# Two-layer encoder in float32 on one core: the first head group kept on chip through the paired gate projections and rotated behind them, and stored gates loaded two at a time on the weights' queue

## The chip, the cores and the metric

The kernel runs on one core of one Trainium2 chip. The metric is the device time of one execution in microseconds (us). The engines are named as in the profile: PE (TensorE, matmuls), PEld (its weight loads), DVE (VectorE), ACT (ScalarE), POOL (GpSimd) and SP (SyncE, which here only issues transfers).

## The reference

An encoder trunk of two layers on 512 tokens of width 2048; 16 meta tokens go ahead of them, so 528 rows are worked on. Only layer 0, attention, is touched by the change.

```python
def attention_mixer(h, w_in, q_norm, k_norm, w_out, ang_row, ang_col):
    proj = h @ w_in
    q, k, v, gate = jnp.split(proj, [...], axis=-1)
...
    q = apply_axial_rope(rmsnorm(q, q_norm), ang_row, ang_col)
    k = apply_axial_rope(rmsnorm(k, k_norm), ang_row, ang_col)
...
    s = jnp.einsum('bqkgd,bskd->bkgqs', qb, k) * (ATTN_HEAD_DIM ** -0.5)
    p = jax.nn.softmax(s.astype(jnp.float32), axis=-1).astype(v.dtype)
    o = jnp.einsum('bkgqs,bskd->bqkgd', p, v)
...
    return (o * jax.nn.silu(gate)) @ w_out

for i in range(2):
    y = rmsnorm(h, pre_norm[i])
    y = attention_mixer(...) if i == 0 else gla_mixer(...)
    h = h + rmsnorm(y, post_norm[i])
return h[:, 16:]
```

There are 16 query heads of 128 in 8 groups; the two heads of a group share one k and one v. A group thus takes four projections of 128 columns (k, q0, q1, v), and each head has a gate projection of 128 columns besides. Layer 1 is a chunked gated linear attention with a gate of its own.

## The kernel before, in words

**Arithmetic.** Every float32 operand is split into a high and a low part (`split`, L128: ACT makes the high part, DVE the low one), and a product is three matmuls (L152 to L154). The normalised rows lie on chip as `uh`, `ul`, features on the partitions and the 528 rows along the free axis, in two halves of 264. A 128-column projection (`project`) is 16 feature tiles by two halves by three matmuls, 96 matmuls of 128x264. Its weights come in two loads of 512 KB on SP's queue into two raw buffers (`weights`, L141) and are split into three pairs `whi`, `wlo`.

**Order.** `Clock` (L38) is a clock for writing the program out: each feature tile of a projection moves it on by 3*(264+7)/2400, some 10.8 for a whole projection, and generators and `clk.after` calls put the other work between at set times. A scheduler then fixes each engine's order from that; loads of weights are drawn ahead of other work.

**Stages.** With x coming in, PE accumulates k, q0 and q1 of group 0 in six PSUM banks, to about 60 us. Then `taken` copies each out, scaled by its norm's weight, and squares it, and `rope` (L297) rotates it, one after the other, with `clk.flush()` between them. `rope` sends four swapped quarters from `qw` to `qs` (L301, on SP), splits the square, multiplies on POOL by cos and sin (L306, L307), sums the square over the partitions by two matmuls on ones for each half into one PSUM bank (L311, L312; its result is taken by DVE at L313), takes the inverse root on ACT, adds and scales on DVE (L318, L319), and splits the result. Under that stand four projections: gates 0 to 2 and v of group 0, all stored in DRAM (`to_dram`). Then `combine` (L193) builds on DVE, in 8 steps, sums of the four quarters of `uh + ul` into `th`, `tl`, and `seven` (L206) makes two gate projections at a time from seven products of such sums instead of eight: five pairs, gates 3 to 12, stored in DRAM. Its first pair is written in another order (`late=True`), which puts a product of plain `u` second.

**Attention.** `attention` takes a group in nine steps (`SLOTS` of clock each): scores and softmax, then transposes, then, by `clk.after`, `weighted` (L659), the product with v into the bank "o". That bank is a pool of one buffer (`ps_o`), and `rope`'s row sums use it too. While a group is attended, the next group's k, q0, q1 and v are projected and rotated (`qkv`); the second half's row sums come 6.5 behind the projection, in `late`. From group 1 on `stored_gates` (L595) brings the two gates of the group before: GpSimd loads one into `gr` (two buffers), DVE multiplies by `rrow` (L604), `silu` takes ACT and POOL (L614), DVE multiplies the result onto the attention's output (L608), and only then comes the second gate's load. The eight groups run from about 230 to 800 us. The output projection and layer 1 follow.

Of the kernel before, what the change touches and what calls it, by code (L numbers as in the profile page):

```python
# [9 lines left out]
F32 = mybir.dt.float32  # L10
# [8 lines left out]
P = 128  # L19
# [14 lines left out]
AHEAD = 400  # L34
SLOTS = (3.8, 3.8, 3.8, 3.8, 3.8, 3.8, 3.8, 2.6)

# [45 lines left out]
def hybrid_encoder(  # L82
# [21 lines left out]
    g_d = scratch.tile([13, P, T], F32, name="g_d")  # L104
    v0_d = scratch.tile([P, T], F32, name="v0_d")
    kq_d = scratch.tile([4, P, T], F32, name="kq_d")
# [98 lines left out]

    def seven(src, c, ys, th, tl, free, late=False):  # L206


# [27 lines left out]
        def add(o, ps, y):  # L236
            V.tensor_tensor(o, ps, y, op=ALU.add)
# [16 lines left out]
        A.copy(y1[:, l], product(w, of_u(0, 0)))  # L254
        if late:
            w = parts(a12)
            A.copy(y2[:, l], product(w, of_u(1, 0)))
        add(y1[:, r], product(parts(a11), of_t(T2)), y1[:, l])
        if late:
            add(y1[:, l], y1[:, l], y2[:, l])  # L260
        add(y2[:, r], product(parts(a21), of_t(T3)), y1[:, r])
# [3 lines left out]
        add(y1[:, r], p5, y1[:, r])  # L265
        if not late:
            w = parts(a12)
        sums(a11, a12, a11)
        if not late:
            add(y1[:, l], product(w, of_u(1, 0)), y1[:, l])  # L270
        add(y1[:, r], product(parts(a11), of_u(1, 1)), y1[:, r])
# [15 lines left out]
    def take(wcol):  # L287

        qw = wk.tile([P, T], F32, tag="qw", name="qw", bufs=2)
        sq = wk.tile([P, T], F32, tag="sq", name="sq", bufs=1 if wk is ws else 2)  # L290

        def evac(ps, a, b):
            A.activation(qw[:, a:b], ps, AF.Copy, scale=wcol)
            A.activation(sq[:, a:b], ps, AF.Square)
        return qw, sq, evac

    def rope(qw, sq, outs, ps_q, tag):  # L297
        qs = wk.tile([P, T], F32, tag="qs", name="qs", bufs=1)
# [8 lines left out]
        G.tensor_tensor(qs, qs, sin, op=ALU.mult)  # L307

        def sums(a, b):
            ps = ps_q.tile([P, 512], F32, tag=tag, name="ssq")[:, :b - a]  # L310
            PE.matmul(ps, ones_r, sh[:, a:b], start=True, stop=False)  # L311
            PE.matmul(ps, ones_r, sl[:, a:b], start=False, stop=True)  # L312
            V.scalar_tensor_tensor(f[:, a:b], ps, 1.0 / P, erow[:, a:b], op0=ALU.mult, op1=ALU.add)  # L313

        def late():
            sums(*HALVES[1])
            rsqrt_inplace(f)
            V.tensor_tensor(qw, qw, qs, op=ALU.add)  # L318
# [13 lines left out]
    Q1 = T + META  # L332
    qks = [qk_tiles(c0, 0)]

    st = ExitStack()
    sp = pool(st, "start")
    wk = ws = pool(st, "wk_s", 2)
    s2 = pool(st, "start2", 2)
# [136 lines left out]
    V.tensor_scalar(col(QN), col(QN), SCALE, None, op0=ALU.mult)  # L475

    def taken(i):
        qw, sq, evac = take(col(QN if i else KN))
        for j, ps, a, b in banks:
            if j == i:  # L480
                evac(ps, a, b)
        return qw, sq
    head0 = taken(0)

# [12 lines left out]
    rsqrt_inplace(rrow)  # L497
    cos, sin = [ws.tile([P, T], F32, name=n, bufs=1) for n in ("cos0", "sin0")]
    nc.sync.dma_start(out=cos, in_=rope_cos)
    nc.sync.dma_start(out=sin, in_=rope_sin)  # L500
# [14 lines left out]

    def to_dram(dst, i, c):

        y = yp.tile([P, T], F32, tag=f"y{i % 2}", name="y")
        project(w_in0, c, HALVES, lambda ps, a, b: A.copy(y[:, a:b], ps))
        nc.gpsimd.dma_start(out=dst, in_=y)  # L520
    built = clk.drive(combine(th, tl, quarters))
    for i, (dst, c) in enumerate([(g_d[i], 4096 + i * P) for i in range(3)] + [(v0_d, 3072)]):
        to_dram(dst, i, c)
    clk.finish(built)
    free = [wpool.tile([P, 1024], F32, tag="wraw", name="wraw", bufs=2) for _ in range(2)]
    free += [q[:, :1024] for q in quarters]
    for h in range(3, 13, 2):
        ys = y_tiles()
        free = seven(w_in0, 4096 + h * P, ys, th, tl, free, h == 3)
        for i in range(2):  # L530
            nc.gpsimd.dma_start(out=g_d[h + i], in_=ys[i])
# [5 lines left out]
    pk = pool(l0, "pk0")  # L537
    qks.append(qk_tiles(pk, 1))
    pb = pool(l0, "pb0")
# [19 lines left out]
    def values(g):  # L559
        vh = wa.tile([P, 4, P], F32R, tag="vh", name="vh")  # L560
        vl = wa.tile([P, 4, P], F32R, tag="vl", name="vl")
        vm = vm_bufs[g % 2]
        vt = wa.tile([P, T], F32, tag="vt", name="vt", bufs=1)
        if g == 0:
            with tc.high_priority(AHEAD):
                nc.sync.dma_start(out=vt, in_=v0_d)
        else:
            project(w_in0, 3072 + g * P, HALVES, lambda ps, a, b: A.copy(vt[:, a:b], ps))

        def late():  # L570
# [3 lines left out]
            for t in range(4):  # L574
# [22 lines left out]
    def stored_gates(hs, held):  # L597

        yield 6.0
        for h in hs:  # L600
            gr = wa.tile([P, T], F32, tag="gr", name="gr", bufs=2)
            nc.gpsimd.dma_start(out=gr, in_=g_d[h])
            yield 6.0
            V.tensor_tensor(gr, gr, rrow, op=ALU.mult)  # L604
            gs = silu(gr)
            yield 4.0
            og = held[h % 2]
            V.tensor_tensor(og, og, gs, op=ALU.mult)  # L608
            nc.gpsimd.dma_start(out=og_d[h], in_=og)
# [96 lines left out]
    for g in range(KV):  # L706
        o_sb = o_tiles()
        att = attention(qk, vv, o_sb, SLOTS[g])
        att = clk.drive(att)
        gates = [] if g == 0 else [2 * g - 2, 2 * g - 1]  # L710
# [10 lines left out]
        if g + 1 < KV:  # L721
# [6 lines left out]

    slots = [wk.tile([P, T], F32, tag=tag, name="ogr", **kw) for tag, kw in
             (("qw", {}), ("qw", {}), ("qs", dict(bufs=1)), ("sq", dict(bufs=2)))]  # L730
    slots.append(wa.tile([P, T], F32, tag="vt", name="ogr", bufs=1))
    NS = len(slots)
# [696 lines left out]
```

## Time and profile before

| what | value |
|---|---|
| time, median of 3 runs | 1833.05 us (1831.9 to 1833.15) |
| the profiled execution's own time | 1830.58 us |
| its span | 1828.7 us |
| PE busy | 1764.1 us, 96% of the span |
| DVE, ACT, POOL busy | 61%, 52%, 12% |

A row of the timeline gives start, duration, engine, line, operation, output and inputs, shape, count and, in square brackets, how long the engine was idle ahead of it and what ended that. A row of the groups gives busy time, mean ns, and the idle time ahead. A row of the windows gives the window, its length, PE's busy time with its matmuls in brackets, the granted clock (1.00 is full), the share of the transfer engines and GB/s. A row of the waits gives total, times and the longest.

### The profile page before, as it was taken

Reading aid. Unit: us, or ns where it says so; the run is one execution under the profiler, and the core shown is the slowest. Engines: PE = TensorE matmul, PEld = TensorE weight load, DVE = VectorE, ACT = ScalarE, POOL = GpSimd, SP = SyncE. Lnnn points to the kernel's source line nnn. Section 1 sums busy time; section 2 is a strip of 40 time slices with the busy share of each in tenths; the row PEclk is TensorE's granted clock in tenths of the full one; section 3 lists DMA queues with packets and bytes.
Section 4 is the critical chain, followed back from the end, with each engine's and each line's share of the span. In section 5 each row is a group of like instructions: output and inputs, shape, how many; then the busy total and the mean of one; then the engine's idle time right before and its main releaser. Section 6 shows DMA issues by size and latency. Waiting matters only on the chain. (4 is left out here: it accounts for less than half of the span.)

```text
span 1828.7 us, 31700 instructions
## 1 busy us (share of the span) xinstructions
PE 1764.1 (96%) x12591; PEld 1661.6 (91%) x12591; DVE 1118.0 (61%) x1904; ACT 951.1 (52%) x1910; POOL 214.6 (12%) x284
## 2 busy tenths in 40 slices
PE   8969998999989999999999999999999999999998
PEld 8969998999989999999999999998898988888886
DVE  5597765666656666752228697768585775764224
ACT  5633355555555554553237634458575775763221
POOL 3200112122121111021111101110010100000000
PEclk9989999999999999999999999999999999999999
DMA  8334342323232323253335344443332332354323
GB/s 266 115 99 124 113 138 77 87 78 101 66 102 65 88 81 96 72 175 93 93 104 169 118 133 128 125 119 95 87 110 77 102 103 75 104 156 164 101 93 127
DMA packets 266468, 202.03 MB, mean 110 GB/s; under 512 B 9836, under 2 KB 239920, under 8 KB 265792
## 3 DMA queue, kind: packets, MB, share of 16 engines
q1 hardware_dynamic: 255056, 163.33, 30.9%
q0 software_dynamic: 11264, 36.68, 5.8%
q8 instruction: 99, 1.62, 0.4%
q14 instruction: 49, 0.40, 0.1%
HBM read 165.20 MB, written 28.28 MB: 106 GB/s over the span
## 5 line engine op out<-in xcount | busy, mean ns | idle before, releaser
L152 PE MATMUL pp<-uh,whi 128*128 128x264 f32 (+1 forms) x2320 | 713.7, 308 | 3.2 <-DVE gr L620 1.4
L153 PE MATMUL pp<-ul,whi 128*128 128x264 f32 (+1 forms) x2320 | 704.0, 304 | 1.4 <-DVE ul L428 1.4
L154 PE MATMUL pp<-uh,wlo 128*128 128x264 f32 (+1 forms) x2320 | 704.0, 303 | 0.4 <-POOL wlo L367 0.3
L130 DVE TENSOR_TENSOR wlo<-wraw,whi 128x1024 fp32r<-128x1024 f32 (+1 forms) x239 | 293.1, 1228 | 307.8 <-ACT whi L129 306.9
L152 PEld LDWEIGHTS pp<-uh,whi 128*128 128x128 f32 x2320 | 439.1, 189 | 19.8 <-DVE gr L620 1.6
L154 PEld LDWEIGHTS pp<-uh,wlo 128*128 128x128 f32 x2320 | 438.7, 189 | 17.5 <-POOL wlo L367 0.6
L153 PEld LDWEIGHTS pp<-ul,whi 128*128 128x128 f32 x2320 | 439.3, 189 | 15.5 <-DVE ul L428 1.8
L129 ACT CAST whi<-wraw 128x1024 fp32r<-128x1024 f32 (+1 forms) x239 | 248.6, 1041 | 298.0 <-PE pp L153 109.4
L230 PE MATMUL pp<-uh,whi 128*128 128x264 f32 x264 | 75.8, 287 | 13.8 <-ACT whi L129 13.8
L129 ACT CAST whi<-x 128x1024 fp32r<-128x1024 f32 x48 | 50.2, 1047 | 72.6 <-PE pp L231 52.8
L232 PE MATMUL pp<-uh,wlo 128*128 128x264 f32 x264 | 75.7, 287 | 0.0
L1341 PE MATMUL f<-whi,ul 128*128 128x512 f32 x192 | 75.6, 394 | 0.0
L1339 PE MATMUL f<-whi,uh 128*128 128x512 f32 x192 | 75.5, 393 | 0.0
L634 ACT ACTIVATE pn<-s,mx 128x528 f32<-128x528 f32 (+1 forms) x72 | 50.3, 698 | 48.3 <-DVE mx L631 47.5
L231 PE MATMUL pp<-ul,whi 128*128 128x264 f32 x264 | 75.4, 285 | 0.0
L1340 PE MATMUL f<-wlo,uh 128*128 128x512 f32 x192 | 75.3, 392 | 0.0
L130 DVE TENSOR_TENSOR wlo<-x,whi 128x1024 fp32r<-128x1024 f32 x48 | 58.6, 1223 | 20.8 <-ACT whi L129 20.7
L631 DVE TENSOR_REDUCE mx<-s 128x1 f32<-128x528 f32 (+1 forms) x72 | 50.8, 705 | 24.6 <-PE s L628 23.1
L306 POOL TENSOR_TENSOR qw<-qw,cos 128x528 f32<-128x528 f32 x24 | 31.7, 1320 | 276.5 <-DMA qs<-qw 276.5
L230 PEld LDWEIGHTS pp<-uh,whi 128*128 128x128 f32 x264 | 50.3, 191 | 14.0 <-ACT whi L129 14.0
L649 DVE TENSOR_TENSOR pl<-pT,ph 128x512 fp32r<-128x512 f32 (+1 forms) x80 | 47.5, 594 | 22.7 <-ACT ph L648 22.3
L648 ACT CAST ph<-pT 128x512 fp32r<-128x512 f32 (+1 forms) x80 | 40.9, 511 | 37.0 <-PE pT L644 25.8
(399 smaller groups left out, 3714.0 us busy)
## 6 DMA issues: line engine op xcount, KB each, us to landing
wraw<-in_attn_w_in_dram SPq DMA_DIRECT2D x82, 512.0 KB, 4.2
wraw<-in_gla_w_in_dram SPq DMA_DIRECT2D x81, 512.0 KB, 3.9
wraw<-in_attn_w_out_dram SPq DMA_DIRECT2D x32, 512.0 KB, 3.9
wraw<-in_gla_w_out_dram SPq DMA_DIRECT2D x32, 512.0 KB, 3.8
x<-in_gla_w_in_dram SPq DMA_DIRECT2D x15, 512.0 KB, 4.4
qs<-qw SPq DMA_DIRECT2D x96, 66.0 KB, 2.8
x<-in_attn_w_in_dram SPq DMA_DIRECT2D x12, 512.0 KB, 4.2
x<-h_d SPq DMA_DIRECT2D x32, 132.0 KB, 4.0
```

The costliest lines, as they stand in the source:

```text
L129: A.copy(hi, src)
L130: V.tensor_tensor(lo, src, hi.bitcast(F32), op=ALU.subtract)
L152: PE.matmul(ps, wh, uh[:, k, a:b], start=first, stop=False)
L153: PE.matmul(ps, wh, ul[:, k, a:b], start=False, stop=False)
L154: PE.matmul(ps, wl, uh[:, k, a:b], start=False, stop=last)
L230: PE.matmul(ps, w[0][:, k], bh[:, k], start=k == 0, stop=False)
L231: PE.matmul(ps, w[0][:, k], bl[:, k], start=False, stop=False)
L232: PE.matmul(ps, w[1][:, k], bh[:, k], start=False, stop=k == KH - 1)
L631: V.reduce_max(mx, s, axis=AX.XY, negate=True)
L1339: PE.matmul(ps, uh[:, k, ts], wh[:, kk], start=(k == 0), stop=False)
L1340: PE.matmul(ps, uh[:, k, ts], wl[:, kk], start=False, stop=False)
L1341: PE.matmul(ps, ul[:, k, ts], wh[:, kk], start=False, stop=(k == KT - 1))
```

## The change

Group 0's raw k, q0 and q1 are copied from the six banks into three tiles of `c0`, which live through the pairs (`qws`); raw v goes into `vt` there and not to DRAM. The rotation of group 0 leaves the start: `first_group` squares, scales and rotates the three behind the pairs, as a lead-in to the first group's attention, with the row sums 2.6 and 3.9 behind each. The later groups rotate in the same three tiles. Their two row sums are placed apart, at 4.4 and 5.6, and no longer in `late`. Group 1's v is projected ahead of its k. `seven` has one order. The first two groups' slots are 3.0 and 3.5. The two stored gates of a group are both issued at the head of the group, on SP's queue, which also carries the weights. `qs` has two buffers instead of one.

```diff
-SLOTS = (3.8, 3.8, 3.8, 3.8, 3.8, 3.8, 3.8, 2.6)
+SLOTS = (3.0, 3.5, 3.8, 3.8, 3.8, 3.8, 3.8, 2.6)
...
-        qw = wk.tile([P, T], F32, tag="qw", name="qw", bufs=2)
-        sq = wk.tile([P, T], F32, tag="sq", name="sq", bufs=1 if wk is ws else 2)
+        qws.append(qws.pop(0))
+        qw = qws[-1]
+        sq = wk.tile([P, T], F32, tag="sq", name="sq")
...
         def late():
-            sums(*HALVES[1])
             rsqrt_inplace(f)
...
-        clk.after(4.4, lambda: sums(*HALVES[0]))
+        for step, part in zip(steps, HALVES):
+            clk.after(step, lambda part=part: sums(*part))
         clk.after(6.5, late)
...
+    qws = [c0.tile([P, T], F32, name=f"qw{i}") for i in range(3)]
+    vt = c0.tile([P, T], F32, name="vt")
...
-    head0 = taken(0)
+    for i, ps, a, b in banks:
+        A.copy(qws[i][:, a:b], ps)
...
-    for i in range(3):
-        rope(*(taken(i) if i else head0), qks[0][1][i], ps_t, "t")
-        clk.flush()
...
-        clk.after(1.2 if g else 8.0, late)
+        clk.after(1.2 if g else 2.0, late)
...
+        vv = values(g) if g == 1 else None
         for i, c in enumerate((2048 + g * P, 2 * g * P, (2 * g + 1) * P)):
             qw, sq, evac = take(col(KN if i == 0 else QN))
             project(w_in0, c, HALVES, evac)
-            rope(qw, sq, outs[i], ps_o, "o")
-        return qk, values(g)
+            rope(qw, sq, outs[i], (4.4, 5.6))
+        return qk, vv or values(g)
+
+    def first_group():
+        for i in range(3):
+            sq = wk.tile([P, T], F32, tag="sq", name="sq")
+            A.activation(sq, qws[i], AF.Square)
+            A.activation(qws[i], qws[i], AF.Copy, scale=col(QN if i else KN))
+            rope(qws[i], sq, qks[0][1][i], (2.6, 3.9))
+            yield 4.2 if i < 2 else 7.5
 
     def stored_gates(hs, held):
 
+        grs = [wa.tile([P, T], F32, tag="gr", name="gr") for _ in hs]
+        for gr, h in zip(grs, hs):
+            nc.sync.dma_start(out=gr, in_=g_d[h])
         yield 6.0
-        for h in hs:
-            gr = wa.tile([P, T], F32, tag="gr", name="gr", bufs=2)
-            nc.gpsimd.dma_start(out=gr, in_=g_d[h])
-            yield 6.0
+        for gr, h in zip(grs, hs):
+            yield 5.0
             V.tensor_tensor(gr, gr, rrow, op=ALU.mult)
...
-        att = clk.drive(att)
+        lead = first_group() if g == 0 else iter([6.5] if g == 1 else [])
+        att = clk.drive(chain(lead, att))
```

The same change in the engines' orders, at three places. First DVE at the end of the start, before: `x_` are the quarter buffers of `combine`, `qw` the vector being rotated, `wlo` the low part of weights.

```order
L318 TENSOR_TENSOR qw<-qw,qs 128x528
L319 TENSOR_TENSOR qw<-qw,sq 128x528
L130 TENSOR_TENSOR wlo<-wraw,whi 128x1024
L130 TENSOR_TENSOR ql_98<-qw,qh_97 128x512
L130 TENSOR_TENSOR ql_98<-qw,qh_97 128x16
L198 TENSOR_TENSOR x_843<-uh,ul 128x1056
L198 TENSOR_TENSOR x_844<-uh,ul 128x1056
```

The same place now; `rrow` is the copy of the rows' scale that before stood ahead of the first rotation's work.

```order
L130 TENSOR_TENSOR wlo<-wraw,whi 128x1024 x2
L469 TENSOR_SCALAR cols<-cols 128x1
L482 COPY rrow<-mrow 128x512
L483 COPY rrow<-mrow 128x16
L198 TENSOR_TENSOR x_745<-uh,ul 128x1056
L484 TENSOR_SCALAR erow<-rrow 128x528
L200 TENSOR_TENSOR x_745<-x_745 128x528
```

The sums of `combine` (L198 on) now follow the row scale at once; before, the three rotations stood between.

Second, DVE in the third group's attention (376 to 448 us in the profile), where q1 of the fourth group is rotated, before: `gr` is a stored gate, `sq` takes the row sums, `pl` and `pmt` are transposed probabilities.

```order
L608 TENSOR_TENSOR o_sb<-o_sb,gs 128x528
L130 TENSOR_TENSOR sl<-sq,sh 128x528
L649 TENSOR_TENSOR pl<-pT,ph 128x4x128
L651 TENSOR_TENSOR pmt<-pTm,pmt 16x128
L313 SCALAR_TENSOR_TENSOR sq<-ssq,erow 128x264
L604 TENSOR_TENSOR gr<-gr,rrow 128x528
L318 TENSOR_TENSOR qw<-qw,qs 128x528
L313 SCALAR_TENSOR_TENSOR sq<-ssq,erow 128x264
L319 TENSOR_TENSOR qw<-qw,sq 128x528
```

And the same part of the same group now (L306 is now the row sums' line, L590 the gate's multiplication, L310 the adding of `qs`, L594 the product with the gate).

```order
L130 TENSOR_TENSOR sl<-sq,sh 128x528
L594 TENSOR_TENSOR o_sb<-o_sb,gs 128x528
L635 TENSOR_TENSOR pl<-pT,ph 128x4x128
L637 TENSOR_TENSOR pmt<-pTm,pmt 16x128
L306 SCALAR_TENSOR_TENSOR sq<-ssq,erow 128x264
L590 TENSOR_TENSOR gr<-gr,rrow 128x528
L306 SCALAR_TENSOR_TENSOR sq<-ssq,erow 128x264
L310 TENSOR_TENSOR qw_96<-qw_96,qs 128x528
L311 TENSOR_TENSOR qw_96<-qw_96,sq 128x528
```

The second row sum has moved ahead of the adding of `qs`; the gate's multiplication still stands between the two sums. The fourth and fifth groups read the same; in the first two the gate's multiplication now stands behind both sums, and in the last three there is none in either kernel's order.

Third, DVE early in the first group's attention, now (before, nothing is rotated for group 0 there): `qw_94` is k, `qw_95` is q0, `vl` the low part of a group's v.

```order
L130 TENSOR_TENSOR sl<-sq,sh 128x528
L553 SCALAR_TENSOR_TENSOR vl<-vps,rcol,vh 128x128
L310 TENSOR_TENSOR qw_94<-qw_94,qs 128x528
L311 TENSOR_TENSOR qw_94<-qw_94,sq 128x528
L306 SCALAR_TENSOR_TENSOR sq<-ssq,erow 128x264
L130 TENSOR_TENSOR kl_2380<-qw_94,kh_2379 128x528
L306 SCALAR_TENSOR_TENSOR sq<-ssq,erow 128x264
L310 TENSOR_TENSOR qw_95<-qw_95,qs 128x528
L590 TENSOR_TENSOR gr<-gr,rrow 128x528
L130 TENSOR_TENSOR wlo<-wraw,whi 128x1024
```

k's adding of `qs` (L310) stands ahead of both row sums of q0, and a gate's multiplication that belongs to the next group stands behind them.

More of the change, by code (lines that the diff above doesn't have):

```diff
@@ L1 @@
 import heapq
+from itertools import chain
 from contextlib import ExitStack
@@ L104, in hybrid_encoder @@
     g_d = scratch.tile([13, P, T], F32, name="g_d")
-    v0_d = scratch.tile([P, T], F32, name="v0_d")
     kq_d = scratch.tile([4, P, T], F32, name="kq_d")
@@ L204, in combine, with seven @@
             yield 2.4
-    def seven(src, c, ys, th, tl, free, late=False):
+    def seven(src, c, ys, th, tl, free):
         def quarter(t, i, j):
@@ L265, in seven @@
         add(y1[:, r], p5, y1[:, r])
-        if not late:
-            w = parts(a12)
+        w = parts(a12)
         sums(a11, a12, a11)
-        if not late:
-            add(y1[:, l], product(w, of_u(1, 0)), y1[:, l])
+        add(y1[:, l], product(w, of_u(1, 0)), y1[:, l])
         add(y1[:, r], product(parts(a11), of_u(1, 1)), y1[:, r])
@@ L295, in take, with rope @@
         return qw, sq, evac
-    def rope(qw, sq, outs, ps_q, tag):
-        qs = wk.tile([P, T], F32, tag="qs", name="qs", bufs=1)
+    def rope(qw, sq, outs, steps):
+        qs = wk.tile([P, T], F32, tag="qs", name="qs")
         for b in range(4):
@@ L309, in sums @@
         def sums(a, b):
-            ps = ps_q.tile([P, 512], F32, tag=tag, name="ssq")[:, :b - a]
+            ps = ps_o.tile([P, 512], F32, tag="o", name="ssq")[:, :b - a]
             PE.matmul(ps, ones_r, sh[:, a:b], start=True, stop=False)
@@ L475, in hybrid_encoder @@
     V.tensor_scalar(col(QN), col(QN), SCALE, None, op0=ALU.mult)
[L477 to L482, printed above, removed]
-    head0 = taken(0)
+    for i, ps, a, b in banks:
+        A.copy(qws[i][:, a:b], ps)
     V.reduce_sum(ss, ssq, axis=AX.X)
@@ L497, in hybrid_encoder @@
     rsqrt_inplace(rrow)
-    cos, sin = [ws.tile([P, T], F32, name=n, bufs=1) for n in ("cos0", "sin0")]
-    nc.sync.dma_start(out=cos, in_=rope_cos)
-    nc.sync.dma_start(out=sin, in_=rope_sin)
-    for i in range(3):
-        rope(*(taken(i) if i else head0), qks[0][1][i], ps_t, "t")
-        clk.flush()
     st.close()
@@ L514, in y_tiles @@
         return [yp.tile([P, T], F32, tag=f"y{i}", name=f"y{i}") for i in range(2)]
[L516 to L520, printed above, removed]
     built = clk.drive(combine(th, tl, quarters))
-    for i, (dst, c) in enumerate([(g_d[i], 4096 + i * P) for i in range(3)] + [(v0_d, 3072)]):
-        to_dram(dst, i, c)
+    for h in range(3):
+        y = yp.tile([P, T], F32, tag=f"y{h % 2}", name="y")
+        project(w_in0, 4096 + h * P, HALVES, lambda ps, a, b: A.copy(y[:, a:b], ps))
+        nc.gpsimd.dma_start(out=g_d[h], in_=y)
+    project(w_in0, 3072, HALVES, lambda ps, a, b: A.copy(vt[:, a:b], ps))
     clk.finish(built)
@@ L528, in hybrid_encoder @@
         ys = y_tiles()
-        free = seven(w_in0, 4096 + h * P, ys, th, tl, free, h == 3)
+        free = seven(w_in0, 4096 + h * P, ys, th, tl, free)
         for i in range(2):
@@ L537, in hybrid_encoder @@
     pk = pool(l0, "pk0")
-    qks.append(qk_tiles(pk, 1))
+    qks = [qk_tiles(pk, i) for i in range(2)]
     pb = pool(l0, "pb0")
@@ L562, in values @@
         vm = vm_bufs[g % 2]
[L563 to L567, printed above, removed]
+        if g:
             project(w_in0, 3072 + g * P, HALVES, lambda ps, a, b: A.copy(vt[:, a:b], ps))
@@ L726, in hybrid_encoder @@
     last_gs = [gate(14)]
-    slots = [wk.tile([P, T], F32, tag=tag, name="ogr", **kw) for tag, kw in
-             (("qw", {}), ("qw", {}), ("qs", dict(bufs=1)), ("sq", dict(bufs=2)))]
-    slots.append(wa.tile([P, T], F32, tag="vt", name="ogr", bufs=1))
+    slots = qws + [vt] + [wk.tile([P, T], F32, tag=tag, name="ogr") for tag in ("qs", "sq")]
     NS = len(slots)
```

7 lines of the change are left out of this document (removed).

## The prediction

> **What bounds the kernel now.** I read the page first, then the waits of PE, then the rows around the longest of them. The page's busy times say that PE is the resource.
>
> ```profile
> PE 1764.1 (96%) x12591; PEld 1661.6 (91%) x12591; DVE 1118.0 (61%) x1904; ACT 951.1 (52%) x1910; POOL 214.6 (12%) x284
> PE   8969998999989999999999999999999999999998
> ```
>
> PE is busy 96% of the span, and the change takes no matmul away: both programs have the same matmuls by count. So it can only gain what PE waits, and the stretches where PE runs slowly. The waits of PE, longest first:
>
> ```profile
> PE o L664 <- DVE sq L313: 20.5, 7, 4.3
> PE pp L230 <- ACT whi L129: 13.8, 1, 13.8
> PE ssq L311 <- ACT sh L129: 3.0, 2, 1.7
> PE pp L152 <- ACT sq L294: 0.7, 1, 0.7
> ```
>
> Two of these hold most of it: one wait of 13.8 at the first pair, and seven waits in attention, one in each group that projects the next, up to 4.3. (The attention of a group takes some 72 us from 232 on; I call these windows 1 to 8, window 1 being the first group's.) The change touches the places of all four. The first pair, in PE's timeline, where the second product waits:
>
> ```profile
> 112.16 0.28 PE L230 MATMUL pp<-uh,whi 128*128 128x264 f32 x1
> ...
> 129.75 0.59 PE L230 MATMUL pp<-uh,whi 128*128 128x264 f32 x1 [13.79 <-ACT whi L129]
> ...
> 299.38 0.56 PE L664 MATMUL o<-ph,vh 128*128 128x272 f32 x1 [4.32 <-DVE sq L313]
> ```
>
> The projections end at 112.16 and the pair begins; its weights for the second product sit in a buffer that `combine` works in until the end, and `combine` is DVE's. DVE's timeline there, and its groups from 92 to 129.7 us:
>
> ```profile
> 61.80 0.17 DVE L495 COPY rrow<-mrow 128x16 f32<-128x16 f32 x1
> 62.50 0.43 DVE L496 TENSOR_SCALAR erow<-rrow 128x528 f32<-128x528 f32 x1
> 92.49 2.42 DVE L198 TENSOR_TENSOR x<-uh,ul 128x1056 f32<-128x1056 f32 x2
> ```
>
> ```profile
> L130 DVE TENSOR_TENSOR t0l<-x,t0h 128x1056 fp32r<-128x1056 f32 x8 | 9.9, 1252 | 1.1 <-ACT t0h L129 1.1
> L198 DVE TENSOR_TENSOR x<-uh,ul 128x1056 f32<-128x1056 f32 x8 | 9.9, 1250 | 0.0
> L200 DVE TENSOR_TENSOR x<-x 128x528 f32<-128x528 f32 x8 | 5.5, 701 | 0.0
> L202 DVE TENSOR_TENSOR x<-x 128x264 f32<-128x264 f32 x8 | 3.3, 427 | 0.0
> L201 DVE TENSOR_TENSOR x<-x 128x264 f32<-128x264 f32 x8 | 3.3, 426 | 0.0
> L130 DVE TENSOR_TENSOR wlo<-wraw,whi 128x1024 fp32r<-128x1024 f32 x2 | 2.4, 1220 | 0.0
> ```
>
> The reader is to see that DVE has no idle time here (1.1 us in 37): `combine` begins only when the last rotation is done, at 92.5, and its eight steps take 9.9 + 9.9 + 5.5 + 3.3 + 3.3 = 31.9 us.
>
> **1. The first pair.** With the rotations gone, `combine` stands directly behind the copy of `rrow`, at 62.0. In between lie the scaling of `erow`, 0.43, and six splits of projection weights, 6 x 1.22 = 7.3. So `th`, `tl` are done at about 62.0 + 0.4 + 31.9 + 7.3 + 1.1 = 102.7. Three sums of weights, of the same shape as a split of weights and counted like it, and one split (4 x 1.22) bring the first product's low weights to 107.6. PE comes to the pair at 112.16 less what part 2 takes, 108.8. DVE is ahead by about 1 us; I keep 0 to 2 us of wait and take 0.5. It removes 13.8 - 0.5 = 13.3. The low clock behind the wait goes with it, by the windows (granted clock behind the matmuls in brackets):
>
> ```profile
> 105.00:110.00 5.00, 5.00 (x44) 1.00 0.26 87
> 129.70:134.70 5.00, 4.81 (x24) 0.61 0.42 118
> 299.30:304.30 5.00, 4.92 (x22) 0.50 0.00 0
> 372.10:377.10 5.00, 4.91 (x27) 0.66 0.00 0
> 444.00:449.00 5.00, 4.97 (x28) 0.66 0.01 3
> 517.00:522.00 5.00, 4.88 (x22) 0.50 0.00 0
> 589.80:594.80 5.00, 4.97 (x28) 0.66 0.00 0
> 660.70:665.70 5.00, 4.94 (x40) 1.00 0.01 3
> ```
>
> 40 matmuls fit in 5 us behind a wait at clock 1.00 (the last row), so one costs 0.125; 24 ran at 0.61, which is 16 x 0.125 = 2.0 lost. Part 1: -15.3.
>
> **2. The start.** The rotations' row sums waited 3.0 there, and the evacuation of the banks 0.7. The plain copies keep some of the latter: I take -0.4. The transfers of v0, cos and sin go too, but PE waits for none of them. Part 2: -3.4. The order without `late` costs nothing by itself: the plain `u` product moves to its place in the other four pairs, where PE waits for nothing.
>
> **3. The wait in each group.** DVE in window 1, up to the row that frees the bank "o" (298.81), then POOL's rows:
>
> ```profile
> 288.57 0.71 DVE L608 TENSOR_TENSOR o_sb<-o_sb,gs 128x528 f32<-128x528 f32 x1
> ...
> 291.88 0.69 DVE L649 TENSOR_TENSOR pl<-pT,ph 128x512 fp32r<-128x512 f32 x1 [1.98 <-ACT ph L648]
> ...
> 292.92 0.43 DVE L313 SCALAR_TENSOR_TENSOR sq<-ssq,erow 128x264 f32<-128x264 f32 x1
> 296.29 0.71 DVE L604 TENSOR_TENSOR gr<-gr,rrow 128x528 f32<-128x528 f32 x1 [2.94 <-DMA gr<-g_d]
> 298.19 0.71 DVE L318 TENSOR_TENSOR qw<-qw,qs 128x528 f32<-128x528 f32 x1 [1.19 <-POOL qs L307]
> 298.81 0.43 DVE L313 SCALAR_TENSOR_TENSOR sq<-ssq,erow 128x264 f32<-128x264 f32 x1
> ...
> 442.09 0.83 DVE L604 TENSOR_TENSOR gr<-gr,rrow 128x528 f32<-128x528 f32 x1 [3.00 <-DMA gr<-g_d]
> ...
> 659.56 0.71 DVE L318 TENSOR_TENSOR qw<-qw,qs 128x528 f32<-128x528 f32 x1 [4.15 <-POOL qs L307]
> ```
>
> ```profile
> 291.46 1.32 POOL L614 TENSOR_TENSOR gs<-gs,gr 128x528 f32<-128x528 f32 x1 [1.29 <-ACT gs L139]
> 293.08 0.58 POOL L602 DMA_DIRECT2D gr<-g_d  x1 [0.30 <-POOL gs L614]
> ```
>
> Two things lie ahead of the second row sum: the stored gate (2.94 and 3.00, windows 1 and 3) and the swapped part from POOL (4.15 in window 6). The change takes the second sum ahead of the adding of `qs` everywhere, so the second cause is gone. The first stays in windows 3 to 5, where the order keeps the gate's multiplication between the sums. Is its gate loaded earlier? It is issued at the head of the window, but into one of two buffers, which POOL (L614) frees only after the gate before went through ACT, and that needs the buffer freed by L608: the chain 288.57, 291.46, 293.08, 296.29 stands as before. So in windows 3 to 5, with the times of window 1 for theirs: the first sum's result is taken at 292.92 to 293.35; the second sum, now 12 matmuls (1.5 us) behind the first, where before it was 21, waits about 1; the gate ends at 297.0, the second sum's result at 297.4, and the product with v, 18 matmuls (2.25 us) behind the second sum, waits about 1.5. I take 2.5 each (0 if the gate is in early, 4.3 if it is as before); in windows 1, 2, 6 and 7 the rest of a row sum's path, 0.4 to 0.5. The sum is 2 x 0.4 + 3 x 2.5 + 2 x 0.5 = 9.3 for 20.5. Part 3: -11.2.
>
> **4. The clock behind those waits.** By the windows, the waits of windows 1 to 5 were followed by 22 to 28 matmuls where 40 fit: (18 + 13 + 12 + 18 + 12) x 0.125 = 9.1. Window 6's was not (40 at 1.00). With two waits of 1 to 1.5 in place of one, I expect none: part 4 is -9.1. If windows 3 to 5 keep it, (18 + 13) x 0.125 = -3.9 is left.
>
> The Trainium skill (TensorE: Matmul & The Clock Gate, HAM oscillation) puts the bound at PE gaps of some 3.4 us. By that rule only windows 1 and 5, if the latter's wait is as long as the 4.32 of the former (both show 22 matmuls), would pay: part 4 would be about 2 x 18 x 0.125 = -4.5 and the time 1802, inside the forecast's bounds. The trace differs: three windows show 0.66, and 0.66 is neither clock alone, so a shorter wait has cost something there.
>
> **5. The first group's attention (window 1).** Its small waits before, from 230 to 760 us:
>
> ```profile
> PE pTm L646 <- DVE pl L649: 1.0, 1, 1.0
> PE s L626 <- ACT pn L634: 0.8, 1, 0.8
> PE pT L644 <- DVE vm L584: 0.4, 1, 0.4
> ```
>
> They go as the steps start later (-2.2). New there: three rotations, whose k product must be ready when the scores start, some 20 us behind the pairs (by the order, 158 PE instructions on). One rotation needs its swap, two POOL products (2 x 1.32) and two DVE rows (2 x 0.71), 4.1 us and the swap; k's fits well into the 20, all three in a row take 12 and the swaps, and PE's projections are their cover (the next group's four, 384 matmuls at 0.125, 48 us). The DVE order puts k's adding of `qs` ahead of q0's row sums, which share one bank: about 1.4 for q0's second sum, 1 for q1's, 1 for the transposes of v, 1 or so more. I take +5, between 0 (the cover holds) and 12 (each of the six sums and of three score steps late by one POOL product, 9 x 1.32). Part 5: +2.8.
>
> **6. Gate loads among the weights.** Thirteen loads move from POOL's queue to SP's, ahead of the next weight loads.
>
> ```profile
> 305.48 16.58 SPq L147 DMA_DIRECT2D wraw<-in_attn_w_in_dram  x3
> ```
>
> A held gate load would hold what is queued behind it: weights. On before's times the one in the POOL rows (293.08) would stand 12 us ahead of the next weight load (305.48). Zero, because that gap covers it.
>
> **Sum.** -15.3 - 3.4 - 11.2 - 9.1 + 2.8 = -36.2. The profiled execution took 1830.58, so 1794.4; the median of the runs is 1833.05, 2.5 above, so **1797**. A measurement of this kernel can tell about 0.2%, 3.7 us.
>
> **The rivals.**
> A. The waits of part 3 stay, bank and clock with them (parts 3 and 4 at nothing): -15.3 - 3.4 + 2.8 = -15.9, 1817. For it: one bank, and the same gate chain. Against: the swapped part no longer stands ahead of the sum, in seven windows of seven. 0.13. The Trainium skill (Perfetto Trace Analysis, Optimization Strategy) says that a gap repeating on the engine that should be full can mean too few buffers for the next tile; the bank "o" stays single, so that rule is on A's side, and the trace agrees that PE waits for that bank, though a DVE row held by a transfer is what keeps it.
> B. The gates are in early and all of part 3 goes: -20.5 instead of -11.2, 1788. For it: issue at the head of the group. Against: the two buffers. 0.17.
> D. The first group is late: with slots of 3.0 each of nine steps waits for a rotation's two POOL products, 9 x 2.6 = 23 more, 1820. For it: a rotation passes SP, POOL, ACT, DVE and the one bank. Against: PE has projections. 0.10.
> E. DVE is late at the first pair by 9 us more, if the combine steps wait for ACT as well as DVE: 1806. For it: a margin of 1 us. Against: DVE's 1.1 us idle in 37. 0.07.
> C, slower. The gate loads on SP hold the weights: each waits for its `gr` buffer until POOL's product, and behind it PE's projections run out of raw weights. Three buffers of split weights and 12 us of gap cover it; it decides beyond 12 us. If a load is held for 17 us (from the product at 288.57 to the weight load at 305.48), 5 us are exposed, eleven times (the thirteen loads less the first two, whose buffers are free), 55: 1852. For it: SP takes its queue in order. Against: the chain above frees the buffer within 5 us of the product. 0.03.
>
> **How the numbers follow.** The forecast has 0.50. Its own bounds: 0 to 2 in part 1, 3 x (0 to 4.3) in part 3, -4 to -9.1 in part 4, 0 to 12 in part 5, which is 1788 to 1810. With B below and A above, the range is 1784 to 1818; out of it are C, D and the ends. Faster by over 0.2%: all but C and a little, 0.94; the same 0.02; slower 0.04.
>
> **What would show it.** In the profile after: no wait for L129 at the first pair, and `combine`'s first row at about 62 (part 1); the waits for "o" in windows 3 to 5 at 1 to 3, behind a gate's transfer, and small in the others (part 3); granted clock 1.00 behind them (part 4); new waits for row sums, 5 us in all, in window 1 (part 5); SP's weight issues as dense as before (part 6). Wrong if PE's total of waits is above 35 us, if a window shows PE's clock under 0.9 right behind the waits of windows 1 to 7, or if projections wait for weights.

## The result, and the profile after

The changed kernel takes 1801.44 us (median of 4 runs, 1801.33 to 1804.34), the kernel before 1833.1 on the same chip: a ratio of 0.9832, 95% interval 0.9815 to 0.9849. Forecast were 1797, 1784 to 1818. The profiled execution took 1801.33, its span is 1799.6, 29.1 shorter than the span before.

The page after: PE's busy time has fallen by 6.0 us, all the rest of the gain is waits.

```profile
PE 1758.1 (98%) x12591; PEld 1654.9 (92%) x12591; DVE 1128.4 (63%) x1904; ACT 951.3 (53%) x1909; POOL 208.3 (12%) x270
PE   8999899999999999999999999999999999999998
```

PE's waits after, longest first (the first rows of the view):

```profile
PE ssq L304 <- DVE sq L306: 12.8, 7, 5.5
PE o L650 <- DVE sq L306: 5.0, 4, 1.6
PE pt L420 <- DMA xt<-in_x_dram: 2.5, 1, 2.5
PE s L612 <- ACT pn L620: 2.3, 2, 1.4
PE pT L630 <- DVE pl L635: 1.8, 1, 1.8
```

The row of 13.8 at the first pair and the two for `sh` at the start are gone. The row of 20.5 has become two rows of 12.8 and 5.0, of which 7.1 are new and lie in the first group. DVE at the end of the start, and PE at the first pair:

```profile
60.77 0.17 DVE L483 COPY rrow<-mrow 128x16 f32<-128x16 f32 x1
60.85 1.25 DVE L198 TENSOR_TENSOR x<-uh,ul 128x1056 f32<-128x1056 f32 x1
...
96.09 1.26 DVE L130 TENSOR_TENSOR t0l<-x,t0h 128x1056 fp32r<-128x1056 f32 x1
```

```profile
104.79 0.28 PE L154 MATMUL pp<-uh,wlo 128*128 128x264 f32 x1
104.91 0.28 PE L229 MATMUL pp<-uh,whi 128*128 128x264 f32 x1
```

`combine` begins at 60.9 instead of 92.5 and is through at 97.4, 7.5 us ahead of the pair. Where the time went is seen best from three points that both programs have: the first pair's first matmul, the pairs' last one, and one matmul behind the attention (number 6100 of PE's record, counted from 0, at 811.54 before and 782.69 after). The idle time of PE within each stretch is in brackets.

| stretch | before | after | difference | forecast |
|---|---|---|---|---|
| start, to the first pair | 112.16 (10.4) | 104.91 (5.3) | -7.3 | -3.4 |
| the five pairs | 118.74 (13.9) | 102.08 (0.0) | -16.7 | -15.3 |
| attention | 580.64 (27.4) | 575.70 (23.4) | -4.9 | -17.5 |
| the rest, to the last matmul | 1008.35 | 1008.31 | 0.0 | 0 |

Twelve row-sum matmuls (12 x 0.122 = 1.5 us) have moved from the first stretch to the third, and six of the first group's score matmuls (0.7 us) from the second, where they stood at 115.06 to 115.67, to the third. So the time came nearly as forecast in the pairs, a little better at the start, and much of the gain forecast in the attention is missing. The question for the experiments was where that went.

The first group's attention after. PE comes to the row sum of q0's second half at 219.2 and waits 5.48, until DVE has taken the first half's sum out of the bank:

```profile
224.67 0.59 PE L304 MATMUL ssq<-sh,ones_r 128*128 128x264 f32 x1 [5.48 <-DVE sq L306]
225.06 0.42 PE L305 MATMUL ssq<-sl,ones_r 128*128 128x264 f32 x1
...
241.22 0.39 PE L612 MATMUL s<-kh,qh 128*128 128x264 f32 x1 [1.35 <-ACT pn L620]
```

DVE there, POOL, and SP's queue:

```profile
220.77 1.79 DVE L310 TENSOR_TENSOR qw<-qw,qs 128x528 f32<-128x528 f32 x1 [4.33 <-POOL qs L300]
222.66 1.61 DVE L311 TENSOR_TENSOR qw<-qw,sq 128x528 f32<-128x528 f32 x1
224.20 0.42 DVE L306 SCALAR_TENSOR_TENSOR sq<-ssq,erow 128x264 f32<-128x264 f32 x1
```

```profile
218.17 1.31 POOL L299 TENSOR_TENSOR qw<-qw,cos 128x528 f32<-128x528 f32 x1 [9.58 <-DMA qs<-qw]
219.45 1.29 POOL L300 TENSOR_TENSOR qs<-qs,sin 128x528 f32<-128x528 f32 x1
220.70 1.29 POOL L299 TENSOR_TENSOR qw<-qw,cos 128x528 f32<-128x528 f32 x1
221.96 1.75 POOL L300 TENSOR_TENSOR qs<-qs,sin 128x528 f32<-128x528 f32 x1
```

```profile
204.15 1.49 SPq L294 DMA_DIRECT2D qs<-qw  x2
207.04 0.39 SPq L147 DMA_DIRECT2D wraw<-in_attn_w_in_dram  x1
207.48 1.33 SPq L294 DMA_DIRECT2D qs<-qw  x1
212.92 0.37 SPq L147 DMA_DIRECT2D wraw<-in_attn_w_in_dram  x1
213.35 3.13 SPq L294 DMA_DIRECT2D qs<-qw  x5
```

Read from the bottom: k's fourth swap leaves SP only at 213.35, behind a weight load that had itself waited for a raw buffer; POOL's products follow at 218.17; DVE's adding of `qs` (L310) stands at 220.77, and the row that empties the bank (L306, 224.20) stands behind it in DVE's order. Before, all this happened at the start, with four projections under it.

### The profile page after: what moved, and what is told of

Same layout as the page of the kernel before. It is cut to its first block, busy times and chain, and to the rows that moved or that the text cites. A ratio compares the mean times of both kernels' runs of the same rounds, so it can differ in the third digit from the quotient of the medians.

```text
span 1799.6 us, 31638 instructions
## 1 busy us (share of the span) xinstructions
PE 1758.1 (98%) x12591; PEld 1654.9 (92%) x12591; DVE 1128.4 (63%) x1904; ACT 951.3 (53%) x1909; POOL 208.3 (12%) x270
## 4 chain that ended last, share of the span: by engine, by line
PE 81%; DVE 7%; ACT 4%; DMA 3%; issue 2%; POOL 2%; SPq 1%; DVEq 0%; POOLq 0%; ACTq 0%
PE pp L152 15%; PE pp L154 14%; PE pp L153 14%; PE pp L229 4%; PE pp L231 4%; PE pp L230 4%; PE f L1326 2%; PE f L1324 2%; PE f L1325 2%; DVE wlo L130 2%; DMA qs<-qw 1%; ACT whi L129 1%; PE pT L630 1%; PE o L1144 1%; PE o L1145 1%
## 5 line engine op out<-in xcount | busy, mean ns | idle before, releaser
L154 PEld LDWEIGHTS pp<-uh,wlo 128*128 128x128 f32 x2320 | 437.6, 189 | 17.5 <-POOL wlo L361 0.6
L152 PEld LDWEIGHTS pp<-uh,whi 128*128 128x128 f32 x2320 | 437.6, 189 | 17.4 <-POOL whi L360 1.2
L153 PEld LDWEIGHTS pp<-ul,whi 128*128 128x128 f32 x2320 | 438.0, 189 | 13.9 <-DVE ul L422 0.4
L229 PE MATMUL pp<-th,whi 128*128 128x264 f32 x192 | 56.1, 292 | 0.4 <-ACT th L129 0.4
```

The lines of the kernel that those rows point to most:

```text
L152: PE.matmul(ps, wh, uh[:, k, a:b], start=first, stop=False)
L153: PE.matmul(ps, wh, ul[:, k, a:b], start=False, stop=False)
L154: PE.matmul(ps, wl, uh[:, k, a:b], start=False, stop=last)
L229: PE.matmul(ps, w[0][:, k], bh[:, k], start=k == 0, stop=False)
```

## The experiments

Ratios are to the kernel before, measured beside it on the same chip. The changed kernel's is 0.9832; the intervals are some 0.0015 wide to either side, about 3 us. Theory: the gain has four parts (the start, the first pair, the second row sum's place, the clock behind the waits), and the first group's attention gives part of it back. The main rival: the gates, loaded at once, are what shortened the waits in the groups.

**The gates as before.** The changed kernel with

```diff
-        grs = [wa.tile([P, T], F32, tag="gr", name="gr") for _ in hs]
-        for gr, h in zip(grs, hs):
-            nc.sync.dma_start(out=gr, in_=g_d[h])
         yield 6.0
-        for gr, h in zip(grs, hs):
-            yield 5.0
+        for h in hs:
+            gr = wa.tile([P, T], F32, tag="gr", name="gr")
+            nc.gpsimd.dma_start(out=gr, in_=g_d[h])
+            yield 6.0
```

> The changed kernel (1801.4) with the stored gates loaded as in the kernel before: one at a time, on GpSimd's queue. Theory: what freed PE in the groups is the second row sum's place ahead of the adding of qs, and the gate's load still waits for its buffer wherever it is issued; so the gates' move is worth between 0 and 6 us either way: 1796 to 1806, and the waits for row sums and for the bank o stay at some 11 us from 232 us on. Rival: loading both gates at once is what shortened the waits; then they come back towards 20 us, with low clock behind them: 1809 or more.

1801.28, ratio 0.9836 (0.9822 to 0.985). The gates' move is worth nothing that can be told. In this kernel's order the gate's multiplication stands behind both sums, and windows 3 to 5 still wait 1.3 to 1.5 each, now at the second sum:

```profile
493.01 0.39 PE L304 MATMUL ssq<-sh,ones_r 128*128 128x264 f32 x1 [1.46 <-DVE sq L306]
```

where the changed kernel waits twice there, 1.30 and 1.60. It saves some 3.5 us in these three windows and loses 1.6 in the first (7.12 at q0's sum instead of 5.48) and most of the rest in small waits elsewhere.

**The second sum back in its old place**, in the changed kernel:

```diff
         def late():
+            if len(steps) < 2:
+                sums(*HALVES[1])
             rsqrt_inplace(f)
...
-            rope(qw, sq, outs[i], (4.4, 5.6))
+            rope(qw, sq, outs[i], (4.4,))
```

> The changed kernel with the second half's row sum of groups 1 to 7 put back to 6.5, ahead of the inverse root. Theory: the waits for the bank o come back (some 20 us in seven windows instead of 11) and part of the low clock behind them: 8 to 18 us slower than the changed kernel, 1809 to 1819. Rival (the gates at once did it): within 4 us of 1801.4.

1811.4, ratio 0.9888 (0.9874 to 0.9903): 10 us slower than the changed kernel, inside the theory's range. The waits for the bank are back, with low clock behind them again in two windows. (The traced execution is the fastest of the four, 1808.33; in it the attention is 4.7 us longer than the changed kernel's.)

```profile
PE o L652 <- DVE sq L306: 13.6, 6, 3.5
```

```profile
497.00:502.00 5.00, 4.75 (x26) 0.66 0.00 0
```

**That line alone**, in the kernel before:

```diff
         def late():
-            sums(*HALVES[1])
             rsqrt_inplace(f)
...
         clk.after(4.4, lambda: sums(*HALVES[0]))
+        clk.after(5.6, lambda: sums(*HALVES[1]))
```

> The kernel before (1833.1) with one thing changed: the second row sum at 5.6 instead of in late. Theory: the seven waits for o fall from 20.5 to under 11 us in all and most of the low clock behind them goes (9.1 by the windows): 1814 to 1823. The start and the first pair's wait of 13.8 stay. Rival (the gates at once did it, or the change's gain is all from the start and the first pair): 1829 or more.

1810.95, ratio 0.9888 (0.9874 to 0.9901): 20.4 us faster than the kernel before, beyond the theory's range, and the largest step in the study for one line. The start and the pairs are as before (112.74 and 118.96); the attention takes 560.17 instead of 580.64, with 14.1 of PE's idle time in it instead of 27.4. Its waits from 232 us on, and the clock behind two of them:

```profile
PE ssq L311 <- DVE sq L313: 6.1, 5, 1.5
PE o L664 <- DVE sq L313: 1.8, 1, 1.8
```

```profile
432.20:437.20 5.00, 4.98 (x40) 1.00 0.20 57
570.90:575.90 5.00, 4.98 (x40) 1.00 0.00 0
```

20.5 us of waits have become 7.9, and no stretch at half clock is left in the attention. This kernel's attention is 15.5 us shorter than the changed kernel's, although both have the sums apart: that is mostly the price of rotating the first group there (step 5 below takes it apart).

**The first group's swaps on GpSimd's queue** (`queue=nc.gpsimd` for its three calls of `rope`).

> The changed kernel with the swaps of the first group's three rotations on GpSimd's queue instead of SP's, where they stand between weight loads. Theory: k's last swap behind a weight load on SP holds POOL's products, those hold DVE's adding of qs, and that stands ahead of the row sums of q0: PE's wait of 5.5 us near 225 us is theirs. Off that queue the wait falls to 2 or less and the low clock behind it goes: 4 to 8 us faster, 1793 to 1797. Rival: the one bank and DVE's pace in the first window set the wait; then the time stays within 2 us of 1801.4.

1799.57, ratio 0.9829 (0.9815 to 0.9842). The 5.48 is gone from 224.67, but there is a wait of 4.19 at 217.82: in this order k's adding of `qs` stands ahead of k's own sums on DVE, so k's second sum waits for the first to be taken. And the second scores (at 242.65) wait 2.66 instead of 1.35. SP's queue was what held that one row, but not what sets the time: the theory's 4 to 8 us are refuted.

**The first group's sums in other banks** (`ps_t`, two buffers, instead of `ps_o`).

> The changed kernel with the row sums of the first group's three rotations in the two buffers of the transposes (tag t) instead of the single bank o. Theory: at 225 us the bank is held because DVE's row that empties it stands behind DVE's adding of qs, which waits for POOL; with a second bank PE need not wait for it at q0's second sum: the 5.5 us there shrink to 2 or less, 4 to 7 us faster than the changed kernel, 1794 to 1797. Rival: whatever bank, PE's next work (the transposes of v, q1's sums, the scores) waits for the same DVE rows; then the waits only move and the time stays within 2 us of 1801.

1802.48, ratio 0.9838 (0.9824 to 0.9853): no gain, the rival. Waits up to 250 us:

```profile
PE ssq L304 <- ACT sh L129: 2.5, 1, 2.5
PE ssq L304 <- DVE vm L560: 2.0, 1, 2.0
PE ssq L305 <- DVE sl L130: 0.6, 1, 0.6
```

5.1 instead of 8.5 us, but both longer ones are followed by a slow stretch, where there was one:

```profile
214.30:219.30 5.00, 4.99 (x28) 0.66 0.72 188
228.20:233.20 5.00, 4.32 (x20) 0.55 0.56 149
```

**All row sums in those banks.**

> The changed kernel with all row sums in the two buffers of the transposes. If the single bank o is what costs the remaining waits in the middle windows (2.9 us each by the trace after), they go, together with those of the first window: 10 to 15 us faster than 1801, 1786 to 1791. If the transposes then wait for those two banks in their stead, within 3 us of the run with the first group's sums alone moved, or slower.

1805.58, ratio 0.9856 (0.9841 to 0.9871), some 4 us slower than the changed kernel. The waits for "o" are gone, and the transposes and the sums wait for each other's banks in their stead: `pTm` for the row sums 5.4 us, the sums for `pl` 4.7. So giving the sums two banks that they share with the transposes does not help; a second bank for the sums alone was not tried. What empties the bank is late in either case.

**The second sum late and the gates as before together.**

> The changed kernel with the second row sum back at 6.5 and the gates loaded one at a time by GpSimd: of the attention's windows only the three raw tiles and the two buffers of qs stay changed. With the sum late alone the waits for the bank o were 13.6 us, against 20.5 in the kernel before. If the gates loaded at once made that difference, the waits go back to 18 to 21 us and the time to 1815 or more; if the two buffers of qs made it, it stays within 3 us of 1811.

1812.95, ratio 0.9896 (0.9881 to 0.9911), the bank's waits 13.9: as with the sum late alone (13.6). The gates make no difference here either. So of the fall from 20.5 to 13.6, something else in the change has taken 7. The traces say where: in windows 3 to 7 these waits came to 13.1 in the kernel before, and to 12.7 and 12.8 in the two kernels with the sum late; in windows 1 and 2 they fell from 7.4 to 1.0 and 1.1 (waits of 0.4 to 1.1 for other rows came there). The two buffers of `qs` serve all windows alike and are an unlikely cause; the shorter first slots, the lead-in and v ahead of k touch the first two windows alone. Which of these it was is not shown.

**`combine` 10 us later**, by eight additions of 128x1056 ahead of it, in the changed kernel:

```diff
+    for _ in range(8):
+        V.tensor_tensor(quarters[3].rearrange("p (j t) -> p j t", j=2),
+                        *[t[:, 0:KH + 1:KH].bitcast(F32) for t in (uh, ul)], op=ALU.add)
     built = clk.drive(combine(th, tl, quarters))
```

> The changed kernel with eight more additions of 128x1056 on DVE ahead of combine (8 x 1.25 = 10 us of work that nothing uses). It tests the first step: that the wait of 13.8 us at the first pair went because DVE starts combine earlier. By the margin of about 1 us in the prediction, 9 us of wait come back, and some low clock: 1810 to 1812. By the trace after, where DVE is done with the sums some 4 us ahead, 5 to 7: 1806 to 1809. If DVE's start is not what the first pair waits for, 1801.

1805.66, ratio 0.9853 (0.9837 to 0.987). No wait came back at the first pair beyond 0.2 us, from 60 to 212 us:

```profile
PE pp L229 <- ACT whi L129: 0.2, 1, 0.2
```

The pairs took 104.13 instead of 102.08, 2.1 more, with four transposes of v now among them. So both margins (1 us, and 4 us from the trace after) were too small: of 10 us at least 8 were covered. In this run DVE's last split of `combine` ends at 117.0, 11 us after the pair began (105.81): the pair did not need all of `combine` at its start, as the prediction had it. Another 2.0 us lie in the attention (577.74 instead of 575.70); why, the trace does not say. That DVE's start sets the first pair is not shown by this run; for it speak only the traces before and after, where the wait went together with the earlier start.

**The rotations further apart**, 6.0 instead of 4.2. In the next three kernels the third rotation works on the tile that holds k, and not q1: the list of tiles has been turned once by then. They leave out the first group's rotation of q1; their times stand for the same amount of work with another dependence.

> The changed kernel with the first group's three rotations 6.0 apart instead of 4.2, and the first scores at the same place (4.0 behind the third instead of 7.5). Theory: the 8.5 us of waits in the first window, and the low clock behind the longest, come from PE meeting q0's row sums before k's rotation has left DVE; with more projection work between, the wait of 5.5 falls to 2 or less: 4 to 8 us faster, 1793 to 1797. Rival: the waits move to the scores or to q1's sums, as they did when the sums got other banks: within 2 us of 1801.

1805.04, ratio 0.9854 (0.9838 to 0.9871). The wait at q0's sum is 6.01 and not under 2.

> As e9, and the gates loaded as before the change (one at a time, GpSimd's queue). There DVE's order has the gate's multiplication behind both row sums in every window, and the waits of the middle windows were 1.3 to 1.5 instead of 1.9 to 3.0. Theory: 2 to 4 us faster than e9, 1790 to 1795, the fastest so far. Rival: the gates' move is worth nothing here as well: equal to e9.

1802.14, ratio 0.9834 (0.982 to 0.9849): 4.68 there.

> As e9, and the first group's swaps on GpSimd's queue. If weight loads on SP hold the swaps and that still costs something once the rotations are spread, 1 to 4 us faster than e9; if not, equal to it.

1801.66, ratio 0.9834 (0.9819 to 0.9849): 3.69 at 218.33, and attention of 572.74. None of the three is told apart from the changed kernel for the better; with another tile in the third rotation they say little on the spacing, and the way to a cheaper first group stays open.

**One order of the pairs in the kernel before** (`late` off).

> The kernel before with its first pair in the order of the other pairs (late off), which the change also does. The prediction put this at nothing. Theory: the first pair waits for combine, so in this order the second product waits for the sums' last part instead: a wait of 12 to 15 us at the first pair, 1830 to 1835. Rival: the late order itself put a load into a buffer that combine held, and so part of the 13.8 us belongs to it: 1820 to 1828.

1826.73, ratio 0.997 (0.9957 to 0.9983). PE's waits at the pair and in the groups:

```profile
PE o L664 <- DVE sq L313: 19.4, 7, 4.0
PE pp L230 <- ACT whi L129: 10.8, 1, 10.8
```

The wait is 10.8 instead of 13.8 and the pairs take 116.03 instead of 118.74. So the late order cost some 3 us by itself in the traces, and 6.2 by the medians (3 to 8 by the interval): the rival. Most likely it is the buffer: the late order's second product needs the weights of `a12`, which are loaded into one that `combine` uses nearly to its end. (In this order the wait is at a product with `t0h`.)

## Why the prediction was right, step by step

The time lies 4.4 us above the forecast, inside the range. The number came nearer than its parts. The sum was made for the profiled execution, 1794.4, and that took 1801.33, 6.9 more; the 2.5 added for the median are luck, since after the change the median lies next to the profiled execution. And apart from the moved matmuls the attention gained 7.1 of the 17.5 forecast; the start and the pairs gave back 3.1 of the missing 10.4. (The prediction's own bounds, all taken at once, come to 1784 to 1816 and not to 1788 to 1810.) The steps:

1. **The first pair**, -15.3 forecast, -16.7 + 0.7 = -16.0 measured in the pairs. Right in mechanism: `combine` at the start, no wait, full clock. Wrong in two details that made no difference, because no wait was left: the margin of 1 us was at least 8, since `combine` was done at 97.4 and not at 102.7 (it began at 60.85, and DVE's rows overlap a little: the next begins 1.17 us on, where the row lasts 1.25) and the pair does not need all of it at once; and "the order without `late` costs nothing" misses that it gains 3 us in the kernel before.
2. **The start**, -3.4 forecast, -7.3 + 1.5 = -5.8 measured. The waits named went; the other kernels with the same start reach the first pair at 105.62 to 107.01, so 1 to 2 us of this is scatter.
3. **The waits in the groups**, 20.5 to 9.3 forecast; 12.8 + 5.0 - 7.1 (the first group's own) = 10.7 measured. Right in the middle windows, with the split at 1.30 and 1.60 in window 4 as worked out. There a gate's transfer holds the second sum, as forecast:

```profile
488.76 0.43 DVE L306 SCALAR_TENSOR_TENSOR sq<-ssq,erow 128x264 f32<-128x264 f32 x1
491.49 1.57 DVE L590 TENSOR_TENSOR gr<-gr,rrow 128x528 f32<-128x528 f32 x1 [2.30 <-DMA gr<-g_d]
492.98 0.42 DVE L306 SCALAR_TENSOR_TENSOR sq<-ssq,erow 128x264 f32<-128x264 f32 x1
```

But the second sum did not move ahead of the adding of `qs` "everywhere": in windows 2 and 7 it still stands behind it, and window 7 kept its wait (1.30, before 1.34; forecast 0.5):

```profile
694.73 0.43 DVE L306 SCALAR_TENSOR_TENSOR sq<-ssq,erow 128x264 f32<-128x264 f32 x1
698.12 0.71 DVE L310 TENSOR_TENSOR qw<-qw,qs 128x528 f32<-128x528 f32 x1 [2.96 <-POOL qs L300]
698.75 0.43 DVE L306 SCALAR_TENSOR_TENSOR sq<-ssq,erow 128x264 f32<-128x264 f32 x1
```

That the gates' move brings no time that can be told is shown by two runs, and that the sum's place does most of it by two others; in windows 1 and 2 the rest of the change shortens these waits too.
4. **The clock**, -9.1. Together with step 3 this was -20.3, and the line alone in the kernel before gave -20.4. In the changed kernel the slow stretches of windows 1 to 5 are gone, but two others came, behind the wait of 5.48 and behind a wait of 1.82 late in the attention:

```profile
224.60:229.60 5.00, 4.93 (x30) 0.71 0.23 54
```

```profile
732.20:737.20 5.00, 5.00 (x29) 0.66 0.28 108
```

By the 40 that fit, they cost (10 + 11) x 0.125 = 2.6. The second of these waits goes with the gates. All eight kernels that load them at once wait 1.80 to 1.82 at this place, the three with the gates as before 0.98 or 0.99, and the kernel before 0.97. With the gates at once a product that waits for POOL stands ahead of the row that PE waits for:

```profile
729.66 1.80 DVE L706 TENSOR_TENSOR o_sb<-o_sb,gs 128x528 f32<-128x528 f32 x1 [2.20 <-POOL gs L600]
731.38 0.68 DVE L635 TENSOR_TENSOR pl<-pT,ph 128x512 fp32r<-128x512 f32 x1
```

The size was also somewhat too large: PE's time in the attention apart from its waits fell from 580.6 - 27.4 = 553.3 to 560.2 - 14.1 = 546.0 with the line alone, 7.2. In the changed kernel it is 575.7 - 23.4 = 552.3, with 2.2 of moved matmuls in it: of the 7.2 some 3.2 are left, 2.6 are the two new stretches, and some 1.5 were not traced. Against the 9.1 forecast 5.9 are missing, more than in any other step. The prediction's own sign of being wrong, a clock under 0.9 right behind a wait of windows 1 to 7, showed once: the 0.71 above, in window 1.

5. **The first group**, +2.8 forecast. This step was mis-sized too, and the clock lost behind its waits was left out of it. Its waits are 1.63 + 5.48 + 1.35 = 8.5 where 5 were taken (0 to 12), and there is low clock behind the longest. Against the kernel with the sums apart alone, the changed kernel's attention is 15.5 longer: 2.2 of matmuls moved there, 23.4 - 14.1 = 9.3 of waits, some 4 of slow clock and smaller things. Of the 9.3, some 6.5 are the first group's (8.5 for 2.0) and about 4 windows 3 to 5, where the gate's multiplication still stands between the sums (7.8 for 3.8); elsewhere the waits are about 1 shorter. The step's "cover" was PE's projections, 48 us of them; but the row sum stands early in PE's stream, and PE stood still for 5.48 us with all that work behind it. What held it (a swap behind a weight load on SP, POOL, two DVE rows) is shown by the rows; that taking away one link, the queue or the bank, moves the wait and does not remove it, is shown by two runs.
6. **The gate loads among the weights**, 0. Right; PE waits for no weights.

The rivals: A is refuted by the waits, B by the 10.7 that stay, C by step 6, E by the trace, which has no wait at the first pair. D named the right place at far too high a price: the first group cost some 5 us more than was taken (8.5 - 5 of waits, 1.3 of clock), not 23.

The Trainium skill's rule of a gap of 3.4 us (TensorE: Matmul & The Clock Gate, HAM oscillation) does not hold here as a bound: 1.82 at 732 us was followed by a slow stretch, 1.60 at 493.55 was not (clock 1.00 from 494.20 on). Nor does the length of a wait alone decide in these runs: 2.49 in the kernel before was not followed by one (the prediction's row at 660.70), and the wait of 1.80 to 1.82 in window 8 was in five of the eight kernels that have it. By that rule the prediction worked out 1802. (It names windows 1 and 5; the second window with 22 matmuls is 4, whose wait was 4.20.) That this lies next to the measured time is chance: with the line alone PE's time apart from waits fell by 7.2 and not by 4.5, and what the changed kernel lost of it again was lost behind other waits. Its rule on repeating gaps and too few buffers (Perfetto Trace Analysis, Optimization Strategy) was tried in part only: with the transposes' two banks for all sums the kernel was 4 us slower than the changed one.

## What to carry to other kernels

A reduction that needs a shared bank should be emptied by a row that stands ahead of any row waiting for a slower engine: here one line's place was worth 20 us, and moving whole stages 10 more on top of it. Work moved off a stage where an engine idles is paid for where it lands, so work out the new place in the stream's order, not by how much cover there is. Gains need not add: the line alone gave 20.4, the rest of the change without it about 20, and both together 31, for both shorten the waits of windows 1 and 2.

## What the runs showed of the hardware

DVE's rows of 128x528 with two inputs took 1.79 and 1.61 us at 220.77 and 222.66, where the median of either line's 24 rows is 0.71; each began while one of POOL's products ran (220.70 to 221.99, 221.96 to 223.71). POOL's product at 221.96 took 1.75 instead of 1.3. The Trainium skill (SBUF — State Buffer, on the two separate sides) says that a DVE row with two SBUF inputs and a GpSimd operation lock each other out of a shared port pair; the rows agree with it. The two other rows of these lines that last over 0.8, 1.77 at 234.83 and 1.41 at 355.43, overlap a product of POOL's as well (234.70 to 236.03, 354.95 to 356.27). In the kernel before, none of the 48 rows of the same two lines lasted over 0.71. It cost the first group some 2 us (1.79 + 1.61 - 2 x 0.71), on the chain that PE waited for.
